# The pooling branch's projection as seven-product units ahead of the third branch's gates

## The chip, the cores and the metric

The kernel runs on one core of one Trainium2 chip. The metric is the device time of one execution in microseconds (us); lower is better. A profiled execution gives the trace that the text reads; three executions without a change give the time before. Engine names are those of the profile: PE (matmul), PEld (weight loads), DVE, ACT, POOL and SP (whose main task here is to issue DMAs).

## The reference, cut to what matters

One layer of a hybrid encoder for 512 tokens of width 1024, in float32: a normed input, one wide projection for three token mixers and three gates, three branch projections merged by the gates, an output projection, then a gated feed-forward part.

```python
h = rms_norm(x, norm_mix)
proj = h @ w_in          # columns: u_pool, u_lru, q, k, v, three gates, 1024 each
# A) pooling: four groups of 256 channels, windows 2, 4, 8, 16
for g, w in enumerate((2, 4, 8, 16)):
    ug = u_pool[..., g * 256:(g + 1) * 256]
    cs = cumsum(ug, axis=1)
    mean = (cs - shifted(cs, w)) / minimum(pos, w)
    p[g] = mean - ug
y_pool = concat(p[g] @ w_pool[g]) * pool_scale
# B) y_lru: short convolution, two gates, linear recurrence over the tokens
# C) y_sb: stick-breaking attention, 8 heads of 128
merged = sum(sigmoid(gate[b] + b_gate[b]) * (y[b] @ w_branch[b]) for b in range(3))
x = x + merged @ w_out
x = x + (silu(h2 @ w_ffn_gate) * (h2 @ w_ffn_up)) @ w_ffn_down     # h2 = rms_norm(x)
```

## The kernel before

Channels lie on partitions and tokens along the free dimension. Every float32 product is made of three matmuls: each operand is split into a rounded high part and the low rest, and high x high, high x low and low x high are summed in PSUM. Splitting a weight piece of 128 x 1024 (`split_w`, lines 134 to 143) takes one copy on ACT (the high part, `whi`) and one subtraction on DVE (the low part, `wlo`); three buffers of each rotate. `specs` lists all weight pieces in the order of use, and `weights` (line 297) keeps three pieces ahead of the product that is being written.

There are two forms of a projection. The direct one (`chan_chunk`, line 392) takes 256 output columns in two halves of the inner dimension, each with 24 matmuls of 512 columns. The other one splits inner dimension, tokens and output channels in two each, so that a product of 2 x 2 blocks takes seven block products instead of eight. Their names are "11", "12", "S1" to "S4" and "22"; "S" pieces are sums of blocks of the weight, and the matching sums of the normed input (`T1` to `T4`, `prepare_t`, line 561) are made once. A block product of this form (`product`, line 310) is 24 matmuls of 256 columns into one half of a PSUM tile; partial results are copied out by ACT between products (a "snap") and completed by a DVE sum.

The order of the stages: gates of branch 0; recurrence projections with the gates of branch 1; then v, k and q as seven-product units (`VKQ`); two seven-product units of the third branch's gates (lines 897 to 923, PSUM tiles `ps_gy` and `ps_gx`); then the second part of the kernel, whose tiles reuse the memory and PSUM of the first part. It holds the pooling projection in direct form (`pool_chunk`, four groups in the order 1, 0, 3, 2; PSUM `ps_pool`), the back products of pooling (`pool_back`, with `w_pool`), branch 1 and branch 0 (`branch`, PSUM `ps_br`), and the eight attention heads. Then come the third branch as two seven-product units with their products interleaved (`BORDER`, PSUM `ps_bY` and `ps_bX`), the output projection and the feed-forward part.

The heads are cut into tasks in a list (`abg`, line 1192: 52 places, five for each new head). `tick` (line 356) takes the next task of that list and one or two of a background list (`bg`: pooling of a group, its back products). `half_chunk` ticks once after each 12 matmuls, so the 16 + 16 + 20 ticks of the pooling projection, branch 1 and branch 0 carry the heads. In the pooling branch `evac_u` copies a projected group out of PSUM, `pool_mean` makes the window means by a scan (line 998) and subtracts the token (line 1001), `split_hl` splits the result, and `pool_back` multiplies.

The framework plans the order of instructions on each engine itself: it takes the instructions that its own cost estimate holds to be ready, by priority, and then fixes that order. `high_priority` raises a priority, `issue_after` adds an order between two instructions. On each engine the planned order is then run as it stands. A DMA issued by Pool with `accum_op=ALU.add` adds what it reads from HBM onto a tile in SBUF; the q and gate units (line 215), the third branch (line 270) and the down projection use it to make the weight sums.

`q_scales` (line 811) makes the scales of the queries on POOL, after product "12" of the second gate unit in program order. `b4` gives tiles of the first part by tag: eight "w" buffers hold the blocks of the seven-product units, as each unit's loads are issued while the previous unit is running (`seven_load`). `mp` holds four tiles "m", first for the input sums, later for the merged rows. The normed input lies in `HH` and `HL`; the same buffers take the recurrence branch's rows (line 1217) once all reads of the input are over.

```python
    def tick(n=1):
        for _ in range(n):
            if abg:
                abg.pop(0)()
            for _ in range(1 + (len(bg) > 8 and "many" in state)):
                if bg:
                    bg.pop(0)()
...
        load_pool_weights(0)
        for g in POOL:
            pool_chunk(g)
        queue_pool_back(POOL[3])
```

## Time and profile before

| | |
|---|---|
| time, median of 3 runs | 867.95 us (867.0 to 869.79) |
| profiled execution | 867.94 us, of which the span of the trace is 866.1 |
| PE busy | 859.3 us, 99% of the span |
| DVE busy | 735.4 us, 85% |
| ACT busy | 523.1 us, 60% |
| POOL busy | 91.1 us, 11% |
| granted TensorE clock | 1.0 |
| moved by DMA | 154.08 MB, 178 GB/s on average |

Busy time is the union of an engine's instructions. Ends of matmuls are modelled, so that a matmul shown with 379 ns overlaps the next one; the pitch of a run of matmuls is read from the chain, where consecutive pieces are merged with their count and their time. In the rows of a stage the columns are the stretch, its length, and each engine's busy time with its instructions, then the granted clock, the share of the 16 DMA engines' time and GB/s. In a time line the bracket at the end of a row tells how long the engine had been idle before it, and what ended that.

### The profile page before, as it was taken

The page shows a single profiled execution, that of the slowest core. Times are in us where ns is not written, and L with a number is a line of the kernel's source. Part 1 is how long each engine was busy: PE and PEld are TensorE (multiplying, and loading weights), DVE is VectorE, ACT ScalarE, POOL GpSimd, SP SyncE. Part 2 cuts the span into 40 slices and gives each one's busy share as a digit, 9 for nine tenths or more (in the row PEclk, how much of TensorE's full clock was granted, in tenths as well). Part 3 has the DMA queues.
Part 4 walks back from the last instruction along what each step waited for, and adds up shares of the span by engine and source line. Part 5 has one row for each costly group of instructions (what it writes and reads, how often), then busy time and mean ns, then how long its engine had stood idle before and what let it go on. Part 6 is the DMA issues. An engine that isn't in the chain of part 4 may idle for free.

```text
span 866.1 us, 14232 instructions
## 1 busy us (share of the span) xinstructions
PE 859.3 (99%) x5563; PEld 790.0 (91%) x5563; DVE 735.4 (85%) x937; ACT 523.1 (60%) x727; POOL 91.1 (11%) x130
## 2 busy tenths in 40 slices
PE   9999999999999999999999999999999999999998
PEld 7888878888899988889889988889999999999998
DVE  7899897998796598967898786699988888899974
ACT  6554989556966567546665545465555555755642
POOL 1110002132433101000001100000000000121200
PEclk9999999999999999999999999999999999999999
DMA  9586346899592876735726955345533433797913
GB/s 340 160 284 208 101 156 186 225 315 264 172 313 74 240 222 195 243 119 157 222 87 169 202 165 172 101 139 148 159 110 98 122 99 123 225 243 195 197 42 122
DMA packets 116643, 154.08 MB, mean 178 GB/s; under 512 B 8160, under 2 KB 90080, under 8 KB 116576
## 3 DMA queue, kind: packets, MB, share of 16 engines
q1 hardware_dynamic: 103904, 107.30, 38.8%
q0 software_dynamic: 12528, 45.62, 22.2%
q8 instruction: 43, 0.70, 0.3%
q10 hardware_dynamic: 144, 0.26, 0.1%
q14 instruction: 24, 0.20, 0.1%
HBM read 132.71 MB, written 18.87 MB: 175 GB/s over the span
## 4 chain that ended last, share of the span: by engine, by line
PE 92%; ACT 4%; DVE 2%; issue 1%; DMA 0%; SPq 0%; DVEq 0%; ACTq 0%
PE ps_y L315 11%; PE ps_q L828 8%; PE ps_x L315 8%; PE ps_dy L1677 6%; PE ps_dx L1677 5%; PE ps_br L306 3%; PE ps_br L308 3%; PE ps_br L307 3%; PE ps_gate L731 3%; PE ps_bY L1301 2%; PE ps_gy L315 2%; PE ps_bX L1301 2%; PE ps_gx L315 2%; PE ps_pool L306 2%; PE ps_pool L307 2%; PE ps_pool L308 2%
## 5 line engine op out<-in xcount | busy, mean ns | idle before, releaser
L141 ACT ACTIVATE whi<-raw 128x1024 fp32r<-128x1024 f32 x69 | 72.8, 1055 | 81.7 <-PE ps_br L307 17.1
L142 DVE TENSOR_TENSOR wlo<-raw,whi 128x1024 fp32r<-128x1024 f32 x69 | 84.2, 1220 | 25.6 <-ACT whi L141 25.0
L142 DVE TENSOR_TENSOR wlo<-qw,whi 128x1024 fp32r<-128x1024 f32 x48 | 58.4, 1220 | 17.0 <-ACT whi L141 17.0
L141 ACT ACTIVATE whi<-qw 128x1024 fp32r<-128x1024 f32 x48 | 50.3, 1053 | 26.4 <-PE ps_q L828 11.9
L1462 ACT ACTIVATE wh_S<-w_S 128x1024 fp32r<-128x1024 f32 x36 | 38.4, 1066 | 28.6 <-PE ps_y L315 20.0
L1583 POOL DMA_DIRECT2D dw<-in_w_down_dram x20 | 17.0, 864 | 305.3 <-DVE wl L1463 242.6
L1463 DVE TENSOR_TENSOR wl_S<-w_S,wh_S 128x1024 fp32r<-128x1024 f32 x36 | 43.8, 1218 | 3.3 <-ACT wh_S L1462 3.3
L1462 ACT ACTIVATE wh<-w 128x1024 fp32r<-128x1024 f32 x27 | 28.6, 1060 | 29.3 <-PE ps_x L315 9.4
L1463 DVE TENSOR_TENSOR wl<-w,wh 128x1024 fp32r<-128x1024 f32 x27 | 32.9, 1219 | 7.8 <-ACT wh L1462 7.8
L1462 ACT ACTIVATE whdS<-dw 128x1024 fp32r<-128x1024 f32 x20 | 21.2, 1062 | 20.3 <-PE ps_dy L1677 10.6
L1113 DVE TENSOR_TENSOR_SCAN E<-K,ahead 128x512 f32<-128x512 f32 (+3 forms) x32 | 25.4, 813 | 5.7 <-ACT K L1109 5.6
L1463 DVE TENSOR_TENSOR wldS<-dw,whdS 128x1024 fp32r<-128x1024 f32 x20 | 24.2, 1220 | 4.9 <-ACT whdS L1462 4.9
L306 PE MATMUL ps_lru<-HH,whi 128*128 128x512 f32 x64 | 24.6, 384 | 0.0
L306 PE MATMUL ps_br<-yph,whi 128*128 128x512 f32 x64 | 24.5, 383 | 0.0
L306 PE MATMUL ps_pool<-HH,whi 128*128 128x512 f32 x64 | 24.5, 383 | 0.0
L306 PE MATMUL ps_br<-yHH,whi 128*128 128x512 f32 x64 | 24.5, 383 | 0.0
L306 PE MATMUL ps_gate<-HH,whi 128*128 128x512 f32 x64 | 24.4, 381 | 0.0
L307 PE MATMUL ps_lru<-HL,whi 128*128 128x512 f32 x64 | 24.3, 379 | 0.0
L308 PE MATMUL ps_lru<-HH,wlo 128*128 128x512 f32 x64 | 24.3, 379 | 0.0
L307 PE MATMUL ps_gate<-HL,whi 128*128 128x512 f32 x64 | 24.3, 379 | 0.0
L308 PE MATMUL ps_gate<-HH,wlo 128*128 128x512 f32 x64 | 24.3, 379 | 0.0
L307 PE MATMUL ps_pool<-HL,whi 128*128 128x512 f32 x64 | 24.3, 379 | 0.0
(740 smaller groups left out, 3437.2 us busy)
## 6 DMA issues: line engine op xcount, KB each, us to landing
raw<-in_w_in_dram SPq DMA_DIRECT2D x31, 512.0 KB, 5.2
qw<-in_w_qkv_dram SPq DMA_DIRECT2D x24, 512.0 KB, 6.9
dw<-in_w_down_dram POOLq DMA_DIRECT2D x20, 512.0 KB, 8.5
w<-in_w_ffn_gate_dram SPq DMA_DIRECT2D x36, 256.0 KB, 3.7
w<-in_w_ffn_up_dram SPq DMA_DIRECT2D x36, 256.0 KB, 4.6
raw<-in_w_branch_dram SPq DMA_DIRECT2D x16, 512.0 KB, 4.4
qw<-in_w_qkv_dram POOLq DMA_DIRECT2D x12, 512.0 KB, 7.6
qd<-r POOLq DMA_DIRECT2D x12, 512.0 KB, 7.2
```

What stands on the lines that cost most here:

```text
L141: act(hi, raw, AF.Copy)
L142: los.append(dve.tensor_tensor(lo, raw, hi.bitcast(F32), ALU.subtract).ins)
L306: nc.tensor.matmul(ps, lh, rh, start=start, stop=False, skip_group_check=skip)
L307: nc.tensor.matmul(ps, lh, rl, start=False, stop=False, skip_group_check=skip)
L308: nc.tensor.matmul(ps, ll, rh, start=False, stop=stop, skip_group_check=skip)
L315: nc.tensor.matmul(o, a_[a][:, w, k, :], il2(b_[b][:, k, :]), start=first and n == k == 0, stop=last and n == 2 and k == 3, skip_group_che ...
L731: nc.tensor.matmul(pss[n // 2][n % 2], w[:, k % 2, n * P:(n + 1) * P], il(hu[k][x_]), start=k == 0 and w is wh and x_ == 0, stop=k == KT - ...
L828: nc.tensor.matmul(ps[:, a, :], b_[:, k, ts_], il(a_[:, kk, :]), start=first and n == k == 0, stop=n == 2 and k == 3, skip_group_check=True)
L1301: nc.tensor.matmul(o, ah[x_][:, w, k, :], il2(b[k][y_]), start=first_ and n == k == 0, stop=n == 2 and k == 3, skip_group_check=True)
L1462: act(h, src, AF.Copy)
L1463: dve.tensor_tensor(l, src, h.bitcast(F32), ALU.subtract)
L1677: nc.tensor.matmul(o, a_[a][:, w, k0 + k, :], il2(b_[b][:, k, :]), start=first and i == k == 0, stop=last and i == 2 and k == nk - 1, skip ...
```

## The change

The pooling projection leaves the second part. It becomes two seven-product units (512 output columns each) that run between q and the third branch's gates, with a layout of its weights made outside the kernel (`w_pool7`). All of its weight sums are made by adding DMAs in place: a unit loads blocks 11, 21, 12 and 22, Pool adds 22 onto 21 (piece S1), then 21 onto 11 after 11's split (S3), 11 onto S1's buffer after S1's split (S2), and 12 onto that after S2's split (S4). The order of products is 11, S1, S2, 12, S3, S4, 22.

The blocks of both units are fetched during q, in place of those of the gate units, which are now fetched during the second pooling unit. The projected rows go to the four "m" tiles and are pooled there in place; `pool_mean` works on 2 x 512 rows and uses a small tile of zeros in place of the `ahead` tile. The second part begins with the split of the pooled rows and the eight back products, with one tick after each. Branches 1 and 0 then tick once after the first 12 matmuls of a half and twice after the next (`TICKS`), so that the heads lie beside these two branches alone.

```diff
+TICKS = (1, 2)
-    def add_pool(g):
-        add_chunk256(("pool", g), w_in, g * 256)
...
             if last:
-                if un < 3:
+                if un == 2:
+                    pool_load(*{"S1": (0, "11", "21"), "S3": (0, "12", "22"), "S4": (1, "11", "21"),
+                                "22": (1, "12", "22")}.get(nm, ()))
+                elif un < 3:
                     seven_load(un + 1, {"S1": ("21",), "S3": ("11",), "S4": ("12",), "22": ("22",)}.get(nm, ()))
...
+    PORDER = ("11", "S1", "S2", "12", "S3", "S4", "22")
+    PNEXT = {"11": ("11", "21"), "S1": ("21", "11"), "S2": ("21", "12")}
+    def pool_load(u=0, *nms):
+        for nm in nms:
+            praw[u, nm] = r = b4([2, 4, P], f"pw{u}{nm}", "w")
+            nc.sync.dma_start(r, pool_src(u, nm))
+            if nm == "21":
+                nc.gpsimd.dma_start(r, pool_src(u, "22"), accum_op=ALU.add)
+    def add_pool7(u, nm):
+        def make(n):
+            parts = split_w(praw[u, {"S1": "21", "S2": "21", "S3": "11", "S4": "21"}.get(nm, nm)], [P, 2, 4, P], n)
+            if nm in PNEXT:
+                buf, m = PNEXT[nm]
+                nc.gpsimd.dma_start(praw[u, buf], pool_src(u, m), accum_op=ALU.add)
+            if u:
+                seven_load(3, {"11": ("21", "11"), "S2": ("12",), "S3": ("22",)}.get(nm, ()))
+            return parts
+        specs.append((("p7", u, nm), make))
...
     for n, (u, pieces, _) in enumerate(UNITS):
+        if n == 3:
+            for cc in range(2):
+                for nm in PORDER:
+                    add_pool7(cc, nm)
         for nm in ORDER:
             for i in range(pieces):
                 add_seven(n, nm, i)
-    for c in POOL:
-        add_pool(c)
...
-            tick(nticks)
+            tick(nticks[j] if type(nticks) is tuple else nticks)
...
+        for cc in range(2):
+            lo, hi = slice(0, H), slice(H, S)
+            Y = pb.tile([P, 2, S], F32, tag="mm", name=f"ps_uy{cc}")
+            X = pb.tile([P, 2, S], F32, tag="mm", name=f"ps_ux{cc}")
+            for j in range(2):
+                upool[cc, j] = mp.tile([P, 2, S], F32, tag="m", name=f"u{cc}{j}")
+            plan = {"11": (Y, 1, True, 0, lo), "S1": (X, 1, True, 1, hi), "S2": (Y, 1, False, 0, hi),
+                    "12": (X, 0, False, None, None), "S3": (Y, 1, False, 1, lo),
+                    "S4": (X, 1, False, None, None), "22": (Y, 0, False, None, None)}
+            for nm in PORDER:
+                ps, half, first_, j, ts_ = plan[nm]
+                product(weights("p7", cc, nm), BQ[WITH[nm]], ps, half, first_, True)
+                if j is not None:
+                    with tc.high_priority(EARLY):
+                        act(two2(upool[cc, j][:, :, ts_]), in_order2(ps[:, :, hi]), AF.Copy,
+                            scale=-1.0 if j else 1.0)
+                elif nm != "12":
+                    j = int(nm == "22")
+                    v = two2(upool[cc, j])
+                    dve.tensor_tensor(v, v, in_order2(ps), ALU.subtract if j else ALU.add)
+                    bg.append(lambda cc=cc, j=j: pool_mean(cc, j))
+                tick(1)
...
-            merge(br, c, chan_chunk(("br", br, c), rhs, 1), gts)
+            merge(br, c, chan_chunk(("br", br, c), rhs, TICKS), gts)
...
-        load_pool_weights(0)
-        for g in POOL:
-            pool_chunk(g)
-        queue_pool_back(POOL[3])
+        for h in range(2):
+            load_pool_weights(h)
+            for g in (2 * h, 2 * h + 1):
+                for j in range(2):
+                    pool_split(g, j)
+        for g in range(4):
+            for j in range(2):
+                pool_back(g, j)
+                tick()
```

70 lines of the change are left out of this document (28 added, 42 removed).

## The prediction

> **What bounds the kernel now.** I read the page's busy shares and chain first, then the stages between the q projection and the third branch's products.
>
> ```profile
> span 866.1 us, 14232 instructions
> PE 859.3 (99%) x5563; PEld 790.0 (91%) x5563; DVE 735.4 (85%) x937; ACT 523.1 (60%) x727; POOL 91.1 (11%) x130
> ...
> PE 92%; ACT 4%; DVE 2%; issue 1%; DMA 0%; SPq 0%; DVEq 0%; ACTq 0%
> ...
> 249.90:287.40 37.50, 37.50 (x337) 37.50 (x337) 26.84 (x25) 24.70 (x30) 11.64 (x11) 1.00 0.47 120
> 287.40:343.40 56.00, 56.00 (x288) 49.76 (x288) 46.19 (x71) 35.17 (x61) 6.74 (x15) 1.00 0.76 231
> 343.40:409.00 65.60, 65.60 (x360) 58.71 (x360) 51.67 (x75) 36.60 (x66) 0.67 (x2) 1.00 0.58 177
> 409.00:468.10 59.10, 58.55 (x317) 51.82 (x316) 53.37 (x102) 35.74 (x78) 3.43 (x4) 1.00 0.52 142
> 287.40:468.10 180.70, 180.16 (x962) 160.28 (x962) 151.24 (x246) 107.52 (x203) 10.83 (x20) 1.00 0.61 182
> ```
>
> The columns of the stage rows are length, then PE, PEld, DVE, ACT, POOL, granted clock, DMA share and GB/s. The rows are the third branch's gates, then the pooling projection, branch 1 and branch 0 with the attention heads among them, and those three together. PE is busy throughout, at full clock; 0.54 us of 180.7 are idle. So a matmul taken away is worth its whole time, until something else is late. The nearest such thing is DVE: 90% busy beside branch 0 (53.37 of 59.10), and PE loses only 0.55 us there.
>
> **The matmuls.** The projection is 192 matmuls of 512 columns now. It becomes 2 units x 7 products x 24 matmuls of 256 columns, 336 in all, in the form that the third branch's gates already have.
>
> ```profile
> L306 PE MATMUL ps_pool<-HH,whi x64: 379/379/463, 287.2 to 341.1; 128*128 128x512 f32 x64
> L307 PE MATMUL ps_pool<-HL,whi x64: 379/379/379, 287.5 to 341.3; 128*128 128x512 f32 x64
> L308 PE MATMUL ps_pool<-HH,wlo x64: 379/379/379, 287.7 to 341.5; 128*128 128x512 f32 x64
> ...
> 239.52 5.18 PE ps_q0S L828 x24
> 260.60 2.68 PE ps_gy L315 x24
> 284.72 2.68 PE ps_gy L315 x24
> ```
>
> In the chain, 24 matmuls of 512 columns take 5.18 us and 24 of 256 take 2.68. So 8 x 5.18 = 41.4 goes and 14 x 2.68 = 37.5 comes: **-3.9 us**. This is the only gain, and all the rest is what can eat it. The Trainium skill ("TensorE: Matmul & The Clock Gate", Back-to-back issue gap) gives N / 2.4 + 2.5 ns, thus an estimate of 109.2 ns at 256 columns and a saving of 4.7 us; the row, 111.7 ns a matmul, decides.
>
> **The sums made by DMA.** In the old form each weight piece was loaded ready. In a new unit, in the order 11, S1, S2, 12, S3, S4, 22, the piece for S2 is S1's buffer after Pool has added block 11 onto it by DMA, and S4's is S2's buffer after block 12. The add may start only when S1's split (ACT, then DVE) has read the buffer, and S2's split starts when it has landed. S3's add follows 11's split and has four products of time: free.
>
> ```profile
> 263.20 1.06 ACT L141 ACTIVATE whi<-qw 128x1024 fp32r<-128x1024 f32 x1 [1.14 <-PE ps_gy L315]
> 264.30 1.23 DVE L142 TENSOR_TENSOR wlo<-qw,whi 128x1024 fp32r<-128x1024 f32 x1 [1.45 <-ACT whi L141]
> ...
> 463.52 0.84 POOL L270 DMA_DIRECT2D bw<-in_w_br_dram  x1 [3.88 <-DVE wlo L142]
> 472.12 1.06 ACT L141 ACTIVATE whi<-bw 128x1024 fp32r<-128x1024 f32 x1 [2.86 <-DMA bw<-in_w_br_dram]
> ...
> 473.08 0.58 ACT L1307 ACTIVATE bt<-ps_bY 128x512 f32<-128x512 f32 x1
> ...
> L215 POOL DMA_DIRECT2D qw<-in_w_qkv_dram x6: 850/870/902, 142.6 to 214.0; - x6
> ...
> DMA to landing us min/median/max: 5.3/6.2/9.4
> ...
> 470.75 5.36 PE ps_bX L1301 x48
> ...
> 502.91 1.08 PE ps_out L372 x5
> 504.70 2.73 PE ps_bY L1301 x24
> ```
>
> A split takes 263.20 to 265.53, 2.3 us. Adds of this kind (the row of line 215, the q and gate units) land 5.3 to 9.4 us after issue, 6.2 at the median; one in the third branch kept ACT until 8.6 us after its issue. From the start of S1's split to S2 being ready: 2.3 + 0.3 to issue (an estimate) + 6.2 + 2.3 = 11.1 us. With three buffers a split starts when the product three places before has ended (the row at 263.20 starts as the product of 260.60 ends), so PE has three products, 8.0 us, meanwhile: 3.1 us are short. From S2's split to S4: the same 11.1 against 2.3 + 8.0 = 10.3, 0.8 short. In the written order that is 3.9 us a unit, 7.8 for both, and 4.4 to 20.6 with the fastest and slowest landing.
>
> But PE is not issued in the written order. At 502.91 matmuls of the output projection run ahead of the last block product (504.70), which is written before them: the planner fills a hole with what it holds to be ready. Product 12, whose block is loaded whole, can go before S2, and 22 or the next unit's 11 before S4. Then 3.1 - 2.7 = 0.4 is left at S2 and nothing to 0.8 at S4. I take 0.6 a unit, **+1.2**, nearer to the planned end because that row shows the planner doing it; 0 to 7.8 stays for the range. The Trainium skill ("DMA: Bandwidth & Descriptors", Anatomy of one DMA) puts a Pool-issued transfer at 2.0 us + bytes / 436e3, 3.2 us for these 512 KB as an estimate; by that nothing would be exposed and the result 1.2 lower. The rows say about twice that.
>
> **What else shares Pool's queue.** The power for q's scales sits in the same stretch:
>
> ```profile
> 256.56 6.38 POOL L342 TENSOR_TENSOR qrs<-qss,mhalf 128x32 f32<-128x32 f32 x1 [2.84 <-DVE qss L814]
> ```
>
> The first gate product starts 2.7 us x 4 before the row at 260.60, at 249.9; S1 of the first unit would split one q piece earlier (12 matmuls, 2.6), at 247.3, S2 at 247.3 + 8.8 = 256.1, and S2's add wants to go at 258.7. Behind the power it goes at 262.9: up to 4.2 late, of which a displaced product covers 2.7 or more. I take **0**, bound 4.2. The q stores and gate-block adds queued there are not on PE's path. SP's loads change owner, not number (eight blocks are fetched during q either way).
>
> **DVE around the projection.** The new form splits 14 pieces instead of 8, adds four 1024-wide sums from PSUM, and does all pooling in this stretch instead of among the heads.
>
> ```profile
> L142 DVE TENSOR_TENSOR wlo<-raw,whi 128x1024 fp32r<-128x1024 f32 x22 | 26.9, 1223 | 16.7 <-ACT whi L141 16.4
> L891 DVE TENSOR_TENSOR gx<-gx,ps_gx x2: 1220/1220/1221, 266.0 to 284.8; 128x1024 f32<-128x1024 f32 x2
> L1001 DVE SCALAR_TENSOR_TENSOR up<-pw,up 128x512 f32<-128x512 f32 x8 | 5.5, 685 | 0.1
> L998 DVE TENSOR_TENSOR_SCAN pw<-up,pw 128x504 f32<-128x504 f32 x2 | 2.5, 1268 | 0.1
> L998 DVE TENSOR_TENSOR_SCAN pw<-up,pw 128x508 f32<-128x508 f32 x2 | 2.5, 1273 | 0.0
> L998 DVE TENSOR_TENSOR_SCAN pw<-up,pw 128x496 f32<-128x496 f32 x2 | 2.5, 1251 | 0.1
> L995 DVE TENSOR_TENSOR pw<-up 128x511 f32<-128x511 f32 x2 | 1.4, 678 | 0.0
> ```
>
> 14 x 1.22 + 4 x 1.22 + pooling 5.5 + 7.5 + 1.4 = 36.4 us of DVE against 37.5 of PE. With the gates behind (26.84 of 37.50) it is 63.2 of 75, 84%: pooling runs over into the gates, splits have priority, **0**.
>
> **The heads beside branches 1 and 0 only.** DVE keeps 151.2 - 8 x 1.22 - 14.4 = 127.0 us there, while PE's 180.7 becomes 139.3: 91%, next to the 90% of the branch 0 row. At its rate of idling, 139.3 x 0.55 / 59.1 = 1.3 less the 0.5 lost now: **+0.8**. The bounds: 0, and DVE filled no better than beside the pooling projection (46.19 of 56.00, 82%): 127 / 0.82 = 155, +15.5. That end is unlikely, since DVE idled there for want of work.
>
> **The joint after the gates.** The pooling chunks that cover it now are gone.
>
> ```profile
> L980 ACT ACTIVATE wph<-rawp x4: 614/629/651, 290.1 to 345.4; 128x512 fp32r<-128x512 f32 x4
> L976 SPq DMA_DIRECT2D rawp<-in_w_pool_dram x2: 373/376/379, 126.5 to 326.1; - x2
> ...
> 332.46 0.55 POOL L1217 DMA_DIRECT2D yHL<-ydl  x1 [39.28 <-PE ps_pool L308]
> DMA to landing us min/median/max: 5.9/6.6/9.0
> ```
>
> The pooling weights lie loaded from 126.5 on, yet their first split runs at 290.1, 2.7 us after the gates' last matmul (287.4): the slots of the second part come free only then. The first group's back products need two weight and two activation splits, 4 x 0.63 on ACT and a last 0.7 on DVE: 5.9 us after the joint. Branch 1's first half covers 5.2 (24 matmuls), because its rows are reloaded once the normed input's first half is read for the last time (the row at 332.46 is that reload; now it can go some 15 us before the joint). The second half's reload waits for S4 and lands 5.9 to 9.0 after: 3.6 to 6.7 past the joint. **+0.5**, between 0 and 1.5.
>
> **Sum.** The profiled run is 867.94, its span 866.1 and 1.8 around it; the median of the runs is 867.95, the same. 867.94 - 3.9 + 1.2 + 0.5 + 0.8 = **866.5 us**. Own range 863.5 (nothing exposed, and the 0.5 of idle gone too) to 868.5.
>
> **Rivals.**
> First, the adds in the written order. For it: the row at 472.12 shows ACT standing 2.86 us for an add that came later than planned, and the copy of a product over at 470.75 ran only behind it, at 473.08; here two such adds follow each other in each unit, the first between neighbouring products. Against: in that stage PE never waited. From a chain longer than three products on, it decides: 867.94 - 3.9 + 7.8 + 1.3 = 873.1. Chance 0.19, the case on the slow side.
>
> Second, DVE becomes the bound beside the heads: filled to 86%, halfway between the two rows, 127 / 0.86 = 147.7, 8.4 more than PE's: 867.94 - 3.9 + 8.4 + 1.2 = 873.6. Against: the 90% row. 0.13.
>
> Third, the power holds S2's add: 866.5 + 3.0 = 869.5, between 0 and 4.2. For: its input is there at 256.56, just ahead of that add. Against: another product can stand in. 0.10.
>
> Fourth, the stalls of the first rival slow the clock.
>
> ```profile
> L731 PE MATMUL ps_gate<-hu,whi x64: 379/379/796, 5.5 to 26.8; 128*128 128x512 f32 x64
> ```
>
> At the start a matmul takes 796 ns against 379. If each of two S2 stalls brings one product at that rate, 2 x 2.9 more: 878.9. No stall of that length is in this trace. 0.03. The Trainium skill (the same TensorE page, HAM oscillation) warns of PE gaps above about 3.4 us; no row here tests it.
>
> That the saving itself fails is no rival: count and pitch are both in rows.
>
> **How the numbers follow.** The forecast has 0.55. About 0.3% (2.6 us) is what a measurement of this kernel can tell: faster means below 865.3, slower above 870.5. Of the 0.55, 0.33 lies below 865.3 (next to nothing exposed) and 0.22 above. The rivals give 0.10 to same (0.03, 0.01, 0.06, 0) and 0.35 to slower. The range 863.5 to 874 takes in the first two rivals at their middle prices.
>
> **What would show it.** Right: 336 matmuls of about 112 ns pitch, ACT waiting for an add before S2 but PE idle under 2 us around the projection; product 12 ahead of S2; the attention stage near 141 us with DVE near 90%. Wrong: PE idle of 3 us before S2, POOL's power ahead of an add, PE waiting on DVE among the heads, or a granted clock below 1.

## The result, and the profile after

The changed kernel takes 900.55 us (median of 4 runs, 898.37 to 901.63) where the kernel before takes 867.58: 1.037 times as long (95% interval 1.034 to 1.040), 33.0 us slower. The forecast was 866.5, its range ended at 874.0. The profiled execution is the fastest of the four, 898.37 us with a span of 896.6.

The head of the page, with the shares of the chain:

```profile
span 896.6 us, 14576 instructions
PE 867.5 (97%) x5707; PEld 796.3 (89%) x5707; DVE 745.3 (83%) x947; ACT 528.5 (59%) x733; POOL 96.6 (11%) x139
...
PE 79%; DVE 8%; ACT 5%; DMA 5%; issue 2%; POOL 0%; SPq 0%; DVEq 0%; ACTq 0%; POOLq 0%
```

The rows of the three stages of the change: the two pooling units, the third branch's gates, and the part with the heads (back products, branches 1 and 0), which the last two rows cut in two. The columns are those explained above.

```profile
251.20:303.80 52.60, 42.11 (x337) 41.24 (x336) 30.77 (x40) 19.54 (x23) 16.71 (x18) 0.87 0.78 196
303.80:346.70 42.90, 38.69 (x338) 37.82 (x337) 33.42 (x38) 23.60 (x29) 6.09 (x11) 1.00 0.50 133
346.70:498.30 151.60, 143.62 (x768) 124.12 (x769) 125.22 (x207) 94.72 (x186) 6.75 (x13) 0.99 0.61 182
...
346.70:376.70 30.00, 26.75 (x116) 21.79 (x117) 17.41 (x26) 16.21 (x26) 3.25 (x9) 0.94 1.03 315
376.70:498.30 121.60, 116.87 (x654) 102.33 (x653) 107.81 (x182) 78.51 (x161) 3.50 (x4) 1.00 0.51 149
```

DVE, ACT and DMA now hold 18% of the chain, where PE alone held 92% before. By the forecast's matmuls the stages should take 37.5, 37.5 and 139.3 us. They take 52.6, 42.9 and 151.6: **15.1, 5.4 and 12.3 us too long**. Less the 3.9 us of matmuls saved that is 28.9 of the 30.5 us between the spans. Of the rest 1.3 is there before q has ended, where nothing was changed (the first product behind q starts between 248.9 and 251.3 in the traces of this study).

In each row length less PE busy is idle time: 10.5, 4.2 and 8.0 us. PE is also busy beyond its matmuls, by 4.6, 1.2 and 4.8 us (42.11 less 37.5, 38.69 less 37.5, 143.62 less 138.8, which is the 180.16 of before less the projection's 41.4). A part of that is matmuls at a lower clock: 3.8 us in the units (worked out below), none in the gates, where the clock is 1.00, and about 1.6 behind them (26.75 us of PE at 0.94). That is 5.4 of 32.8 us, a sixth of the loss. Of the rest a part is only how waits show: a matmul ahead of a wait has its whole modelled length to itself, which otherwise overlaps the next one.

**The first stall.** Pool's time line in the first unit; the two L249 are 11's add and S1's, in this order, behind the second unit's add of 22 (L242) and a q store:

```profile
250.90 0.88 POOL L242 DMA_DIRECT2D pw<-in_w_pool_dram  x1 [7.30 <-DMA pw<-in_w_pool_dram]
251.49 1.02 POOL L811 DMA_DIRECT2D qd<-r  x1
252.21 2.12 POOL L249 DMA_DIRECT2D pw<-in_w_pool_dram  x2
...
255.36 5.45 POOL L369 TENSOR_TENSOR qrs<-qss,mhalf 128x32 f32<-128x32 f32 x1 [0.29 <-DVE qss L844]
```

Two pieces of the chain, the landing of S1's add and the matmuls of S2:

```profile
252.79 10.46 DMA pw<-in_w_pool_dram
...
265.71 4.39 PE ps_uy L342 x22
```

ACT's time line there, and PE's:

```profile
254.04 0.60 ACT L957 ACTIVATE u<-ps_uy 128x512 f32<-128x512 f32 x1 [0.23 <-PE ps_uy L342]
263.34 2.95 ACT L142 ACTIVATE whi<-pw 128x1024 fp32r<-128x1024 f32 x3 [8.71 <-DMA pw<-in_w_pool_dram]
266.20 0.58 ACT L957 ACTIVATE u<-ps_ux 128x512 f32<-128x512 f32 x1
```

```profile
264.45 0.58 PE L342 MATMUL ps_uy<-hT2h,whi 128*128 128x256 f32 x1 [7.77 <-ACT whi L142]
```

S1's add lands 10.46 us after issue, ACT waits 8.71 us for it at S2's split, and PE 7.77. Behind that split stand two more, of pieces due later, and S1's copy out of PSUM (266.20). Then the clock is down: 22 matmuls take 4.39 us where 22 at the usual pitch take 2.46. The second unit repeats this with a shorter wait (landing 5.65 us, 22 matmuls in 4.35). The slow clock thus costs 1.9 us in each unit, 3.8 in both.

**The joint behind the gates**, on ACT, then in the chain:

```profile
352.33 1.06 ACT L142 ACTIVATE whi<-raw 128x1024 fp32r<-128x1024 f32 x1 [4.17 <-DMA raw<-in_w_branch_dram]
353.29 1.13 ACT L1049 ACTIVATE wph<-rawp 128x512 fp32r<-128x512 f32 x2
```

```profile
348.45 0.53 POOL gd L925
348.98 8.30 DMA yHL<-ydl
357.32 0.48 PE ps_br L334
```

ACT waits 4.17 us for the third weight piece of branch 1, with the splits for the back products behind it. The last reload of the recurrence's rows is issued behind the store of the gates and lands 8.30 us later.

### The profile page after: what moved, and what is told of

Same layout as the page of the kernel before. It is cut to its first block, busy times and chain, and to the rows that moved or that the text cites. A ratio compares the mean times of both kernels' runs of the same rounds, so it can differ in the third digit from the quotient of the medians.

```text
span 896.6 us, 14576 instructions
## 1 busy us (share of the span) xinstructions
PE 867.5 (97%) x5707; PEld 796.3 (89%) x5707; DVE 745.3 (83%) x947; ACT 528.5 (59%) x733; POOL 96.6 (11%) x139
## 4 chain that ended last, share of the span: by engine, by line
PE 79%; DVE 8%; ACT 5%; DMA 5%; issue 2%; POOL 0%; SPq 0%; DVEq 0%; ACTq 0%; POOLq 0%
PE ps_y L342 11%; PE ps_x L342 8%; PE ps_q L858 7%; PE ps_dy L1710 6%; PE ps_dx L1710 5%; DMA pw<-in_w_pool_dram 3%; PE ps_gate L761 3%; PE ps_bY L1334 2%; DVE wlo L143 2%; PE ps_br L334 2%; PE ps_br L335 2%; PE ps_br L333 2%; PE ps_gy L342 2%; PE ps_bX L1334 2%; PE ps_uy L342 2%
## 5 line engine op out<-in xcount | busy, mean ns | idle before, releaser
L142 ACT ACTIVATE whi<-raw 128x1024 fp32r<-128x1024 f32 x61 | 64.4, 1056 | 73.4 <-PE ps_out L334 15.5
L143 DVE TENSOR_TENSOR wlo<-raw,whi 128x1024 fp32r<-128x1024 f32 x61 | 74.3, 1219 | 25.7 <-ACT whi L142 25.4
L143 DVE TENSOR_TENSOR wlo<-pw,whi 128x1024 fp32r<-128x1024 f32 x14 | 16.6, 1221 | 18.5 <-ACT whi L142 18.5
L334 PE MATMUL ps_br<-yHL,whi 128*128 128x512 f32 x64 | 24.7, 386 | 1.8 <-DMA yHL<-ydl 1.8
L335 PE MATMUL ps_br<-yHH,wlo 128*128 128x512 f32 x64 | 24.5, 383 | 0.0
```

What stands on the lines that cost most here:

```text
L142: act(hi, raw, AF.Copy)
L143: los.append(dve.tensor_tensor(lo, raw, hi.bitcast(F32), ALU.subtract).ins)
L334: nc.tensor.matmul(ps, lh, rl, start=False, stop=False, skip_group_check=skip)
L335: nc.tensor.matmul(ps, ll, rh, start=False, stop=stop, skip_group_check=skip)
```

## The experiments

All kernels derive from the changed one unless said otherwise; line numbers shift by a few. The table gives the median of 4 runs, the ratio to the kernel before with its interval, and the three stages in the profiled execution, from first matmul to first matmul. The profiled execution can lie some us off the median: it took 912.35 us for distance, 904.50 for the forced order and 896.03 for the DVE sums.

| kernel | us | ratio | units | gates | heads |
|---|---|---|---|---|---|
| changed | 900.55 | 1.037 (1.034-1.040) | 52.6 | 42.9 | 151.6 |
| distance | 905.46 | 1.045 (1.041-1.050) | 59.6 | 41.3 | 162.5 |
| pair | 894.93 | 1.032 (1.030-1.034) | 90.2 together | | 158.3 |
| no pooling | 899.62 | 1.037 (1.036-1.039) | 56.5 | 39.0 | 152.2 |
| queue | 900.26 | 1.039 (1.035-1.042) | 48.7 | 44.6 | 155.9 |
| DVE sums | 893.50 | 1.029 (1.025-1.033) | 42.4 | 43.3 | 157.5 |
| forced order | 908.90 | 1.046 (1.043-1.049) | 59.9 | 40.7 | 155.0 |
| forced, queue | 911.57 | 1.050 (1.048-1.052) | 62.4 | 40.7 | 157.8 |
| other tile | 901.05 | 1.038 (1.036-1.041) | 48.8 | 43.0 | 156.3 |
| other tile, queue | 901.41 | 1.039 (1.037-1.040) | 50.6 | 42.9 | 157.4 |
| place alone | 887.43 | 1.023 (1.022-1.025) | 41.4 | 39.5 | 155.9 |
| heads alone | 873.28 | 1.007 (1.005-1.009) | | 37.5 | 186.5 with projection |
| half | 881.48 | 1.017 (1.015-1.019) | 21.7 | 38.5 | 169.9 with projection |
| joint eased | 900.29 | 1.038 (1.035-1.040) | 52.1 | 44.6 | 153.2 |
| DVE sums, joint | 889.63 | 1.026 (1.023-1.029) | 42.4 | 43.4 | 151.5 |
| DVE sums, joint, fewer loads | 884.77 | 1.020 (1.018-1.021) | 40.5 | 43.4 | 148.0 |
| place, fewer loads | 885.86 | 1.020 (1.017-1.023) | 41.4 | 39.5 | 156.8 |
| place, joint | 884.08 | 1.019 (1.017-1.021) | 41.4 | 39.5 | 151.9 |
| place, joint, fewer loads | 883.92 | 1.019 (1.017-1.021) | 41.4 | 39.5 | 150.2 |

### Distance and pair

```diff
-    PORDER = ("11", "S1", "S2", "12", "S3", "S4", "22")
+    PORDER = ("11", "S1", "12", "S2", "S3", "22", "S4")
```

> The changed kernel (900.5 us) with its products in the order 11, S1, 12, S2, S3, 22, S4: one product whose block comes loaded now stands between S1 and S2 and another one between S3 and S4; nothing else is edited. Theory A (the adding DMAs between neighbouring products are what makes the two pooling units 52.6 us long in place of 37.5, first by the idle time and then by the slow clock behind it): PE has 10.7 us between S1's split and S2 where it had 8.0, the idle time of 8 to 9 us at unit 0 falls to about 5 and that of 3 us at unit 1 to 0 to 1, and with less idle time less of the slow clock: the units take 41 to 46 us and the kernel 889 to 894. Rival A2 (Pool's queue is held by the second unit's add of 22, which waits 7.3 us for its block; the distance between products has little to do with it): unit 0 still idles 6 to 9 us, only unit 1 is mended: 895 to 898. Rival A3 (the stretch is bound by DVE): no gain, 899 to 902.

905.46 us, slower by 5. The experiment did not do what its text says. From the answers for the two PSUM tiles (count, shortest, median and longest duration, first and last start):

```profile
L342 PE MATMUL ps_uy<-hT2h,whi x16: 275/275/581, 261.6 to 298.3; 128*128 128x256 f32 x16
...
L342 PE MATMUL ps_ux<-HH,whi x32: 274/275/481, 265.3 to 308.3; 128*128 128x256 f32 x32
```

Here the first matmul of S2 (hT2h) runs at 261.6, the first of product 12 (HH into ps_ux) at 265.3: the planner put 13 of S2's 24 matmuls ahead of 12 although 12 is written first. PE stands for 7.06 us before S2 all the same. Presumably the planner's own estimate holds the add to have landed by then, so that it sees no hole to fill; the trace does not show the estimate.

The pair takes the third branch's order for both units:

```diff
+    PORDER = ((0, "11"), (0, "S1"), (1, "S1"), (0, "S2"), (0, "12"), (0, "S3"), (1, "11"),
+              (0, "S4"), (1, "S2"), (0, "22"), (1, "12"), (1, "S4"), (1, "S3"), (1, "22"))
```

> The changed kernel with the products of both pooling units interleaved in the order that the third branch uses: 11, S1 of the first unit, S1 of the second, S2, 12, S3 of the first, 11 of the second, S4 of the first, S2 of the second, and so on; the gate units' blocks are loaded as buffers come free. Theory A: every add of the second unit has at least five products of time, the one before S2 of the first unit has one more than it had: one stall is left, of 0 to 5 us, the units take 38 to 45 us, the kernel 885 to 893, at or below the kernel with distance. Rival A2 (Pool's queue): the second unit's add of 22 is needed even sooner here, the first stall stays at 6 to 9 us: 893 to 897. Rival A3 (DVE): 899 to 902.

894.93, 5.6 us less than the changed kernel, above what theory A expected and within the time of rival A2. But the first stall is 2.78 us, not the 6 to 9 of that rival. Units and gates together take 5.3 us less; the last stage takes 6.7 more in the profiled execution, which was the slowest of the four.

### No pooling

```diff
         def pool_mean(cc, j):
+            return
```

> The changed kernel without the window means (pool_mean returns at once: 14 us of scans and subtractions on DVE are left out, and the projected rows go on unpooled). Theory B (the pooling work, held back by the stall, piles up on DVE and makes the gate units 42.9 us long in place of 37.5): the gate units take 37.5 to 39, the units before them stay at 50 to 53, the kernel takes 893 to 896. Theory A alone (the gates are late for want of loads or because of the clock): the gate units stay at 42 to 43, the kernel at 898 to 902.

Its units and gates:

```profile
251.00:307.50 56.50, 43.07 (x337) 42.08 (x336) 24.12 (x23) 19.54 (x23) 16.36 (x18) 0.85 0.74 179
307.50:346.50 39.00, 37.69 (x338) 37.50 (x336) 26.38 (x23) 23.74 (x29) 6.19 (x11) 1.00 0.57 149
```

The gates fall to 39.0, as theory B said, and DVE there from 33.42 to 26.38 us. But the units, in which nothing that PE waits for was touched, took 3.9 us longer in this run (stalls of other lengths), so the total falls by 0.9 only. The pooling work on DVE thus costs about 4 us in the gates. That the stall holds it back, as theory B says, the runs do not bear out: the gates are shortest behind the longest units (40.7 us behind 59.9 and 62.4), and they take 43.3 where most of the stall is gone (the DVE sums below, which also give DVE more work).

### The queue, and the sums by DVE

```diff
-            if nm in PNEXT:
+            if nm in PNEXT and nm != "11":
                 buf, m = PNEXT[nm]
-                nc.gpsimd.dma_start(praw[u, buf], pool_src(u, m), accum_op=ALU.add)
+                add = nc.gpsimd.dma_start(praw[u, buf], pool_src(u, m), accum_op=ALU.add)
+                if nm == "S1":
+                    with tc.issue_after(add.ins):
+                        nc.gpsimd.dma_start(praw[u, "11"], pool_src(u, "21"), accum_op=ALU.add)
+                        if not u:
+                            nc.gpsimd.dma_start(praw[1, "21"], pool_src(1, "22"), accum_op=ALU.add)
```

> The changed kernel with the order of products unchanged, but S1's add (the one that S2 waits for) issued by Pool ahead of 11's add and ahead of the second unit's add of 22, in place of behind both. Theory D (the add lands late because it stands third in Pool's stream of transfers and DMA is full: 10.5 us at the first S2): it lands after 5 to 7 us, the idle time before the first S2 falls from 8 to 9 us to 3 to 5, and with it most of the slow clock behind it: pooling units 45 to 48 us in place of 52.6, kernel 891 to 896. Rival E (the landing is long because all 16 DMA engines are taken by the loads and the q stores, whoever is first): 9 to 11 us to landing again, kernel 898 to 903, and what was put off (11's add, 22's add) may make S3 or the second unit's S1 late: up to 906.

S1's add on Pool, and S2's split on ACT:

```profile
250.38 0.93 POOL L249 DMA_DIRECT2D pw<-in_w_pool_dram  x1 [2.76 <-DVE wlo L143]
```

```profile
256.04 2.00 ACT L142 ACTIVATE whi<-pw 128x1024 fp32r<-128x1024 f32 x2 [2.91 <-DMA pw<-in_w_pool_dram]
```

Issued first, S1's add is there 5.7 us later, where behind two other adds and a q store it took 10.5. That is the landing of theory D, not the 9 to 11 us of rival E. But the add also goes 2.4 us earlier, into a stretch where the DMA engines are less full: their share is 0.74 from 250.4 to 256, and was 0.88 to 1.07 where it took 10.5. The next add of the same run, S4's, goes when Pool has stood idle for 4.8 us, and its split starts 10.2 us later, at a share of 0.91 to 1.06:

```profile
258.65 0.86 POOL L249 DMA_DIRECT2D pw<-in_w_pool_dram  x1 [4.84 <-DVE wlo L143]
```

```profile
268.89 2.95 ACT L142 ACTIVATE whi<-pw 128x1024 fp32r<-128x1024 f32 x3 [5.77 <-DMA pw<-in_w_pool_dram]
```

So place in the queue and full DMA engines are not told apart. The units fall to 48.7. The kernel's time does not fall: gates and heads give it all back (+1.7, +4.3).

```diff
+            if nm == "S4":
+                dve.tensor_tensor(praw[u, "12"], praw[u, "12"], praw[u, "S2"], ALU.add)
             ...
+            if nm == "11":
+                praw[u, "S2"] = r = b4([2, 4, P], f"ps{u}")
+                dve.tensor_tensor(r, praw[u, "21"], praw[u, "11"], ALU.add)
+                nc.gpsimd.dma_start(praw[u, "11"], pool_src(u, "21"), accum_op=ALU.add)
```

> The changed kernel with S2 and S4 summed by DVE out of the loaded blocks, as the gate units do it (four sums of 1024 elements more on DVE, 1.22 us each; the buffer of S1 is left alone; only 22 onto 21 and 21 onto 11 stay adding DMAs). Theory A (the chain of adding DMAs through one buffer, with the slow clock behind its stalls, makes the pooling units 15.1 us too long): units 37.5 to 40, granted clock 1.0 there, gate units 39 to 43 since DVE has 4.9 us more to do: kernel 883 to 889. Rival A3 (DVE is what the stretch is short of): units 45 or more, or all that they win lost again in the gate units: kernel 895 to 902.

Its units, ten microseconds within the gates, then ACT and PE in the first unit:

```profile
251.20:293.60 42.40, 39.72 (x338) 39.31 (x338) 35.23 (x42) 20.13 (x24) 12.99 (x12) 0.96 0.68 193
...
299.00:309.00 10.00, 6.69 (x58) 6.31 (x57) 10.00 (x17) 4.63 (x6) 0.00 (x0) 1.00 0.07 14
```

```profile
260.79 1.06 ACT L142 ACTIVATE whi<-pw 128x1024 fp32r<-128x1024 f32 x1 [3.82 <-DMA pw<-in_w_pool_dram]
261.75 0.58 ACT L960 ACTIVATE u<-ps_ux 128x512 f32<-128x512 f32 x1
```

```profile
262.39 0.38 PE L345 MATMUL ps_ux<-HH,whi 128*128 128x256 f32 x1 [2.42 <-ACT u L960]
```

Without the chain of adds the units take 42.4, 10.2 us less, while the second unit runs without a gap. What is left comes from an adding DMA too. The split that waits 3.82 us is, by its place in the order, S3's: its add was issued at 251.28, 9.5 us before. S1's copy out of PSUM stands behind it on ACT, product 12 waits 2.42 us for that copy, and the clock is down behind it (0.96 over both units). So the chain of theory A has about two thirds of the 15.1 us. The gates stay at 43.3: DVE is full there (10.00 of 10.00 from 299 to 309, PE 6.69).

### The order held to

PE is held to the written order by an order between the last matmul of a product and the first of the next, with the order of the distance run, then with the queue edit as well.

```diff
+                with tc.issue_after(state["mm"]) if "mm" in state else nullcontext():
+                    product(ab, BQ[WITH[nm]], ps, half, first_, True)
```

> The kernel with distance (11, S1, 12, S2, S3, 22, S4), in which PE is held to that order (in the run with distance alone the planner had put 13 of the 24 matmuls of S2 ahead of product 12 in the first unit and 2 in the second, so that PE stood at S2 with 12 ready behind it). Theory A with the planner blind to the wait (its estimate holds the add to be landed, so it sees no hole and fills none): idle time before S2 falls by one product in each unit, to 3 to 5 us and 0 to 2 us; units 44 to 49 us in place of 52.6, kernel 891 to 897. Rival: distance does not help, since S2's add lands as late as it is issued and everything behind it moves along: units 52 to 60, kernel 898 to 906.

> The same forced order, and S1's add issued by Pool ahead of 11's add and of the second unit's add of 22, as in the run that changed the queue alone (there it landed after 5.5 us in place of 10.5). If the two causes of the first stall (no distance, and place in Pool's stream) add up: no stall over 2 us before S2 of either unit, units 38 to 43 us at full clock; what S3 then waits for is 11's add (landing at about 257, S3 due at about 262). Gate units 42 to 45, the stage with the heads 151 to 158: kernel 888 to 894. If they do not: units 46 or more.

908.9 and 911.57: worse, with units as long as the rivals had them (59.9 and 62.4). What PE waited for in the first of them (us in total, times, longest), and ACT there:

```profile
PE ps_ux L342 <- ACT u L959: 11.1, 2, 8.1
```

```profile
260.16 2.00 ACT L142 ACTIVATE whi<-pw 128x1024 fp32r<-128x1024 f32 x2 [7.65 <-DMA pw<-in_w_pool_dram]
262.07 0.58 ACT L959 ACTIVATE u<-ps_ux 128x512 f32<-128x512 f32 x1
```

Product 12 writes the PSUM tile of S1 (ps_ux) and waits for the copy of S1 out of it. That copy (262.07) stands on ACT behind S2's split (260.16), which waits for the DMA. So one wait at the head of ACT's queue holds both S2 and the product that should cover it. It was so in the distance run too (S2's split at 260.45, S1's copy at 262.37): product 12 did not stand ready behind the stall there, although the first expectation above says so. The last two runs of this group put 22 in that place, which writes the other tile:

```diff
-    PORDER = ("11", "S1", "12", "S2", "S3", "22", "S4")
+    PORDER = ("11", "S1", "22", "S2", "12", "S3", "S4")
```

> The changed kernel in the order 11, S1, 22, S2, 12, S3, S4, with PE held to it and the second sum made after S3's copy. The product between S1 and S2 is now one that writes the other PSUM tile: product 12, which stood there in the run with forced order, writes S1's tile, and its first matmul waited for the copy of S1 on ACT, which stands behind S2's split, which waits for the add. Theory K (a wait on ACT's queue also held what should have filled the hole): 22 runs while the add lands, the idle time before the first S2 falls from 8 to 9 us to 4 to 6, before the second S2 from 3 to 0 to 1; units 43 to 48 us in place of 52.6; the kernel 891 to 898. Rival: 22 waits as well, units 52 to 60, kernel 898 to 910.

> The same, and S1's add issued first by Pool, as in the two runs with the changed queue (landing 5.5 to 5.7 us after issue). By theory K both effects add now: the add's split starts at about 256, 22 ends at about 257.3, so S2 waits 0 to 2 us; units 38 to 42 us, clock 1.0 there. Gates 42 to 45, heads' stage 151 to 158: kernel 886 to 893. Rival: as above, 898 to 910.

The first matmul of S2 in the first run; then, in the second, the first of S3, and the split and the copy that it waited for:

```profile
261.23 0.38 PE L342 MATMUL ps_uy<-hT2h,whi 128*128 128x256 f32 x1 [3.56 <-ACT whi L142]
```

```profile
271.61 0.58 PE L347 MATMUL ps_uy<-hT3h,whi 128*128 128x256 f32 x1 [7.75 <-ACT u L964]
```

```profile
270.01 1.06 ACT L142 ACTIVATE whi<-pw 128x1024 fp32r<-128x1024 f32 x1 [9.83 <-DMA pw<-in_w_pool_dram]
270.98 0.58 ACT L964 ACTIVATE u<-ps_uy 128x512 f32<-128x512 f32 x1
```

22 does run while the add lands: the wait before S2 is 3.56 in place of 7.77, and with the queue edit 0.30. Theory K holds for that stall. But then S4's add is the late one, and S3 waits 7.75 us for the copy of S2, which stands behind S4's split on ACT. Units 48.8 and 50.6, the second far from the 38 to 42 expected; the kernels 901.05 and 901.41. The stall moves along the chain, as long as the split of an add that takes 5 to 11 us stands on an engine that also empties PSUM.

### The place without the form, and the heads alone

In the first kernel the projection runs in the new place in the old direct form, pooled in place, all else as changed. The second is the kernel before, with the heads' tasks held back until the last group of the projection.

```diff
-                for nm in PORDER:
-                    add_pool7(cc, nm)
+            for g in range(4):
+                add_chunk256(("pool", g), w_in, g * 256)
...
+            pss = chan_chunk(("pool", g), hn, 1, pb)
+                    act(two(upool[g // 2, j][:, g % 2, :]), in_order(pss[j]), AF.Copy)
```

> The changed kernel with the pooling projection in its new place (between q and the third branch's gates, pooled in place in the same tiles, heads beside branches 1 and 0 only), but in the old direct form: eight weight pieces loaded ready, 192 matmuls of 512 columns, no sums of weights at all. It tells the place from the form. Theory F (the pooling units' 15.1 us come from the form, the stage with the heads is too long because of the place): the projection takes its 41.4 us at full clock, the gate units 37.5 to 41, the stage with the heads 150 to 158 against 139.3: 867.1 + 11 to 19, less nothing, + 0 to 3 = 878 to 889. Rival G (the stage with the heads is long only because what comes before it is late): that stage near 141, kernel 867 to 872.

```diff
-            if abg:
+            if abg and not state.get("hold"):
...
+            state["hold"] = g != POOL[3]
+            pss = chan_chunk(("pool", g), hn, 2 if g == POOL[3] else 1)
...
+            merge(br, c, chan_chunk(("br", br, c), rhs, (1, 2)), gts)
```

> The kernel before (867.6 us) with only the heads moved: no task of the heads runs beside the first three groups of the direct pooling projection, two per half beside the last group, then one and two in turn beside branches 1 and 0, as in the changed kernel. All arithmetic stays. Theory B2 (squeezing the heads beside branches 1 and 0 makes DVE the bound there: the 12.5 us that this stage of the changed kernel takes too long come from it): 876 to 881. Theory C (those 12.5 us come from the joint behind the gates: late reload of the recurrence's rows, splits of the pooled rows): 867 to 870. In the changed kernel's trace PE's idle time is split about evenly, so 872 to 874 would mean both.

Place alone: projection, gates, and the heads' stage in two stretches; then the heads' stretch of the other:

```profile
249.40:290.80 41.40, 41.40 (x193) 36.27 (x192) 21.66 (x30) 12.44 (x15) 9.32 (x9) 1.00 0.59 163
290.80:330.30 39.50, 37.83 (x338) 37.62 (x338) 30.24 (x36) 24.46 (x31) 5.20 (x9) 1.00 0.39 106
330.30:360.30 30.00, 23.50 (x99) 18.84 (x98) 15.29 (x21) 13.31 (x23) 4.19 (x10) 0.89 0.99 309
360.30:486.20 125.90, 121.14 (x674) 105.76 (x673) 111.12 (x186) 81.56 (x166) 3.51 (x4) 1.00 0.52 150
```

```profile
326.20:473.40 147.20, 142.63 (x779) 125.30 (x778) 126.05 (x208) 90.64 (x179) 7.53 (x12) 1.00 0.58 172
```

With no stall ahead, the projection takes exactly 41.40 us and the gates 39.5. The kernel is still 19.9 us slower than before, 16.6 of it in the heads' stage (155.9 against 139.3): 6.5 us idle in the first 30 (30.00 less 23.50), 4.8 in the rest (125.90 less 121.14), and 5.8 that PE is busy beyond its matmuls (23.50 + 121.14 less 138.8), of which 2.6 are the lower clock (23.50 us at 0.89); 0.5 of idle was there before. Theory F holds, G falls. Moving the heads alone costs 6.2 us (873.28 less 867.12), between theories B2 and C, and PE is idle for 4.6 (147.20 less 142.63) there, about as long as in the rest of the place run. That run has no joint, and its clock stays at 1.00.

### Half of the change

```diff
-            for cc in range(2):
-                for nm in PORDER:
-                    add_pool7(cc, nm)
+            for nm in PORDER:
+                add_pool7(0, nm)
...
+    for g in PDIR:
+        add_chunk256(("pool", g), w_in, g * 256)
```

> Half of the change: groups 0 and 1 as one seven-product unit ahead of the gates (sums S2 and S4 by DVE), groups 2 and 3 in the direct form at the head of the second part, with heads beside them again (one tick per 12 matmuls there and beside branch 1, one and two in turn beside branch 0). Matmuls: 1.9 us less than in the kernel before. Theory H (the stage with the heads needs the projection at its head as a cover while its loads, all due at once, keep the DMA engines full for about 30 us; 20.7 us of it cover most of that): the joint costs 0 to 3, the unit 0 to 5 (the first unit of the run with DVE sums lost 4.9): 866 to 874. Rival I (the cost is squeezing the heads, in proportion to the PE work taken from beside them): half of 12 to 18 more, 873 to 880.

881.48, above both ranges (PDIR is groups 2 and 3). The unit loses 2.9 and the gates 1.0, the second part 9.9 against 160.0 (its two groups' 20.7 and 139.3). One wait of a back product is new (us in total, times, longest):

```profile
PE pps L338 <- DVE wtl L1171: 4.5, 1, 4.5
```

It is an order of mine (back products queued behind a head's work), so the run does not tell H from I. Nor does it price half of the place: up to 4.5 of the 9.9 us are that wait.

### The joint

```diff
+            with tc.issue_after(state["psplit"]) if state.get("key") == ("br", 1, 1, 0) else nullcontext():
                 act(hi, raw, AF.Copy)
...
-            nc.gpsimd.dma_start(gd2[cc, j], t)
+            nc.sync.dma_start(gd2[cc, j], t)
```

> The changed kernel with two edits at the joint behind the gates: the split of the third weight piece of branch 1 is put behind the splits of the pooled rows on ACT (in the changed kernel it stands ahead of them and waits 4.2 us for its load), and the gates' results are stored from SP's queue, so that they no longer stand ahead of the last reload of the recurrence's rows on Pool. Theory C (of the 12.5 us that the stage with the heads is too long, about half is idle time at the joint and the slow clock behind it): 4 to 7 us less, 893.5 to 896.5. Rival B2 (all of it is DVE beside the heads, so what the joint gives is taken back behind it): 899 to 902.

900.29: no gain on the changed kernel, whose heads' stage is the shortest of all traces with the old order on ACT. With the sums by DVE:

> DVE sums and the eased joint together. If both causes hold and are separate, the gains add: 900.5 less 11 to 17 less 4 to 7 = 877 to 885, still above the kernel before by about what the heads cost alone (873.3 less 867.1 = 6.2) and what DVE takes in the gates. If one hides behind the other: 884 to 889.

889.63, 3.9 us less than with the sums alone, though the two intervals overlap; each edit gave less than expected. Then loads were left out:

```diff
+                    if 0 < h < 4 and t < 2:
+                        st["raw", t] = state["head0", t]
+                        continue
```

> The kernel with DVE sums and the eased joint (889.6 us), in which heads 1, 2 and 3 use the query and key tiles of head 0: six loads of 256 KB, 1.6 MB of the 9.4 MB that move in the 30 us behind the gates, are left out, and the results of these heads are those of other queries and keys; the instructions of all engines are the same in number. Theory H (the joint is bound by DMA: branch 1's weight pieces and the recurrence's rows land late since everything is due at once): 2 to 6 us less, 883.5 to 887.5, the granted clock behind the joint nearer to 1. Rival J (the joint waits for the order on ACT, DVE and PE, not for bytes): 888 to 891.

> The kernel with the direct projection in the new place (887.4 us), in which heads 1, 2 and 3 use the query and key tiles of head 0 (six loads of 256 KB left out, results of these heads are those of other queries and keys). No sums of weights, no stall and no slow clock come before the joint here. Theory H (joint bound by bytes): 3 to 7 us less, 880.5 to 884.5, granted clock near 1 behind the joint. Rival J (order and latency, not bytes): 886 to 889.

> The kernel with the direct projection in the new place (887.4 us; nothing stalls ahead of the joint) and the joint's order eased as in the earlier run: the splits of the pooled rows go ahead of the waiting split of branch 1's third weight piece on ACT, the gates' results are stored from SP. Theory L (at the joint ACT's order matters: a split that waits 5 us for a load holds the splits that the back products need): the stage with the heads 149 to 152 in place of 155.9, kernel 880 to 884. Rival M (the joint has nothing to run whatever the order: all of branch 1's inputs and weights are on their way): 886 to 890.

> The same, and heads 1, 2 and 3 use the query and key tiles of head 0 (six loads of 256 KB left out, results of these heads are those of other queries and keys). With the unchanged order these loads were worth 1.6 us (887.4 to 885.9), with the eased order and the seven-product form 4.9. If bytes bind once the order is eased: 3 to 5 us below the run with the eased order alone. If not: within 1.5 of it.

884.77 against 889.63 (of which 1.9 in the units), 885.86 against 887.43, and 883.92 against 884.08: fewer bytes gave 4.9, 1.6 and 0.2 us, and only the first is clear of the intervals. The eased order gave 3.4 in the place kernel (887.43 to 884.08), and its heads' stage fell from 155.9 to 151.9, within what theory L expected:

```profile
330.10:482.00 151.90, 142.49 (x770) 124.13 (x769) 126.27 (x207) 95.26 (x187) 5.37 (x10) 0.99 0.63 185
```

So order on ACT has a part in the joint of that kernel; bytes have none that these runs agree on. What stays is latency, and it scatters. The wait of ACT for the third weight piece of branch 1 in the changed kernel was 4.17 us; here the same wait in the run without pooling, the queue run and the run with DVE sums, all with this part of the program unchanged, one fence each:

```profile
353.14 1.06 ACT L142 ACTIVATE whi<-raw 128x1024 fp32r<-128x1024 f32 x1 [5.26 <-DMA raw<-in_w_branch_dram]
```

```profile
351.14 1.06 ACT L142 ACTIVATE whi<-raw 128x1024 fp32r<-128x1024 f32 x1 [6.77 <-DMA raw<-in_w_branch_dram]
```

```profile
346.55 1.06 ACT L142 ACTIVATE whi<-raw 128x1024 fp32r<-128x1024 f32 x1 [8.23 <-DMA raw<-in_w_branch_dram]
```

Waits of 4.17, 5.26, 6.77 and 8.23 us stand beside heads' stages of 151.6, 152.2, 155.9 and 157.5. This stage is where gains of the units went, though the wait goes with its length only roughly (the last run with the queue edit waits 5.84 beside 157.4, the place run 5.15 beside 155.9). Why this load lands later when the units end sooner was not found out.

## Why the prediction was wrong, point by point

- **Matmuls, -3.9:** right. 14 products at the pitch of 24 in 2.68 us, wherever nothing stalls.
- **Sums made by DMA, +1.2:** this step failed. It measured +15.1. Three parts of it were wrong. It took the landing as 6.2 us, the median of adds in q; here S1's add stood behind three other transfers of Pool, in full DMA engines, and took 10.46 (5.7 when first and earlier). The row of line 215 was also the faster half of such adds in the kernel before: its line 200 has a median of 8.7 us and 10.5 at the most, and the page of before gives for all adds of q, and for those of the down projection (KB each, median us to landing):

```profile
dw<-in_w_down_dram POOLq DMA_DIRECT2D x20, 512.0 KB, 8.5
qw<-in_w_qkv_dram POOLq DMA_DIRECT2D x12, 512.0 KB, 7.6
```

  By the forecast's own sum 7.6 us would leave 13.4 for both units, and the slowest landing that it named, 9.4, leaves 20.6; the range took 7.8. The Trainium skill's 3.2 us for such a transfer ("DMA: Bandwidth & Descriptors", Anatomy of one DMA) is below every landing of a weight add seen here (5.2 us at the least); the rows decide. The step let the planner fill the hole; the planner does not see it (the distance run), and where PE was held to another order, the copy behind the waiting split stopped the filler too. Both together are the first rival, but at 7.8 us it was priced without the blocked copy, and without the clock: 3.8 of the 15.1 us are slow matmuls. The fourth rival had the clock, at a chance of 0.03 because "no stall of that length is in this trace"; yet by the forecast's own sum the slowest landing leaves 6.3 us at the first S2.
- **The power on Pool, 0:** right, but by luck. The forecast had the add at 258.7, behind the power, with a displaced product to cover it. The add was issued at 252.79, and the power ran behind it, at 255.36.
- **DVE around the projection, 0:** failed, +5.4 in the gates. The amount was right (63.2 us forecast, 30.77 + 33.42 measured), but an average of 84% over two stages hid a stretch in which DVE is full and PE waits for it:

```profile
310.00:320.00 10.00, 7.51 (x64) 7.32 (x65) 10.00 (x17) 3.91 (x6) 0.00 (x0) 1.00 0.01 2
```

  Without pooling the gates take 39.0, in the place kernel, with 12.3 us less work on DVE in the two stages, 39.5.
- **Heads beside branches 1 and 0, +0.8:** failed. Moved alone they cost 6.2. The 90% of the branch 0 row was an average too; the second rival's 8.4 was nearer.
- **Joint, +0.5:** failed. Joint and heads together cost 12.3 us in the changed kernel and 16.6 in the place run; how much of it is the joint alone stays open. The forecast counted the waits one by one (5.9 against 5.2 us of cover, a reload 3.6 to 6.7 late) and not that these all come at once, on ACT in order, with loads that take 7 to 11 us (the third weight piece is there 7.1 us after issue in the changed kernel, 11.2 with DVE sums) and a clock that falls behind the gap. In the place run, where nothing else is wrong, idle time in the first 30 us is 6.5.

Range and chances followed from prices that were too low at three places, and from a clock that only the fourth rival counted. The place costs 19.9 us by itself, the form 13.1 more (900.55 less 887.43) where it was to save 3.9. None of these kernels beats the kernel before.

## What to carry to other kernels

A stage that runs without a gap on PE may be the cover of everything around it: before it is moved, list what the stage behind it will load and split in its first 30 us, and on which queue in which order. A wait on an in-order engine that also empties PSUM holds the products that should cover it, so a piece that lands late needs an engine, or a place in the order, of its own. Price a PE stall at its length plus the slow matmuls behind it.

## What the runs showed of the hardware

A gap can cost clock even when it is short and broken. In the second unit of the changed kernel PE waits 1.49 us, runs two matmuls, waits 0.77, and 0.9 us later its matmuls take 0.42 us in place of 0.28:

```profile
287.67 0.38 PE L342 MATMUL ps_uy<-hT2h,whi 128*128 128x256 f32 x1 [1.49 <-ACT whi L142]
...
288.93 0.38 PE L342 MATMUL ps_uy<-hT2h,wlo 128*128 128x256 f32 x1 [0.77 <-DVE wlo L143]
...
289.88 0.42 PE L342 MATMUL ps_uy<-hT2h,whi 128*128 128x256 f32 x1
```

In the first unit of the kernel with DVE sums the single wait of 2.42 us is enough (0.96 over both units). In its gates waits of 1.13 and 2.18 us, with 5.6 us of matmuls between them, cost no clock (the row of 299 to 309 above has 1.00, and so have the ten microseconds behind it). The Trainium skill ("TensorE: Matmul & The Clock Gate", HAM oscillation) warns of idle gaps above about 3.4 us. The stall of 7.77 us agrees; the 1.49 and 0.77 us and the 2.42 us are shorter cases than that rule names.
